# The first expert layer of a transformer block: its lower halves off GpSimd, an even pace of the gathers, and the last four output columns without a job queue

## The chip, the core and the metric

One NeuronCore of a Trainium2 chip runs the whole kernel. The metric is the device time in microseconds (us) of one execution. The engines named below are TensorE (PE, its weight loads PEld), VectorE (DVE), ScalarE (ACT), GpSimd (POOL) and SyncE (SP, which here only issues transfers).

## The reference

One block of a diffusion transformer: differential attention and gated linear attention on 256 tokens (with 256 context tokens), merged and added to x, and then an expert feed-forward, on which the change bears. All of it is float32. Cut to that part:

```
def peer_ffn(h, wq, keys, u, v):                       # h: 256 tokens x 2048
    q = (h @ wq).reshape(B, T, 8, 2, 128)
    s = einsum('bthpd,hpkd->bthpk', q, keys)           # 2 x 128 scores a head
    s1, i1 = top_k(s[..., 0, :], 16); s2, i2 = top_k(s[..., 1, :], 16)
    top_s, pos = top_k(s1[..., :, None] + s2[..., None, :], 16)
    idx = take_along_axis(i1 * 128 + i2, pos)          # 8 x 16 of 16384 experts for each token
    g = softmax(top_s)
    act = gelu(einsum('pd,ped->pe', h, u[idx]))        # first layer
    return einsum('pe,ped->pd', act * g, v[idx])       # second layer
out = x + g2 * peer_ffn(...)
```

## The kernel before

**Two ways of doing the experts.** For the first 192 tokens the kernel multiplies all 16384 rows of `u` and `v` as dense matrices (all 128 x 128 experts, 128 blocks of 128 experts), and picks the chosen experts through a matrix `A` of gains, 128 x 128 x 192, zero where an expert was not chosen. For the last 64 tokens it gathers the chosen rows: 64 tokens x 128 experts are 8192 rows, 64 gathers of 128 rows x 2048 numbers.

**The precise product.** A float32 product is made of three products of rounded parts (`fp32r`). Each weight block of 128 x 1024 is loaded by SP (`load_to`, L76) into `wraw`; ACT rounds it into the upper part `whi` (L90), and DVE or GpSimd subtracts to get the lower part `wlo` (L92): `e = nc.gpsimd if self.share(self.s) else nc.vector`. `share` is a function of the block's number. The class `Stream` splits blocks ahead of the matmuls: in the expert layers three blocks ahead, with six `wraw` buffers and four each of `whi` and `wlo`.

**The first layer.** `experts_in(i)` (L1215) does one block of 128 experts, called "one expert block" below: two weight blocks, 16 k-steps of one matmul with `whi` (L1222, 384 columns: upper and lower part of the tokens side by side) and one with `wlo` (L1223, 192 columns), and a fold of the two halves (`summed`: `low` L1234, a matmul L1236, `sum` with the gelu L1241). After every fourth k-step it calls `jobs.tick()`: four ticks in one expert block.

**The order of the work around it.** `Jobs` holds lanes of generators. Each tick takes one off the count of the first generator in every lane; at zero that generator runs to its next `yield`, whose number is the next count. So a lane's work is written into the engines' queues at a fixed pace in matmuls, and each engine then runs its own queue in order. Lanes in this layer:

- `route`: the top-16 searches on DVE, while the first expert blocks run. Until it is empty, `A` does not exist, and `W.share = lambda s: s % 4 != 0` gives three of four `wlo` to GpSimd.
- `gains` (L1264), from the moment the routing is through: 48 steps of four ticks. DVE makes `og` (L1276, four small instructions) and ACT `oh2` (L1272, L1273); two ticks later PE joins them (L1281, eight matmul records), one tick later ACT copies into `A` (L1288).
- `sparse` (`sparse_in`, L1169), from the same moment: 66 steps. Step j multiplies gathered rows j-2 with the tokens and sums (the "dot", L1173 on DVE) and issues gather j on GpSimd (L1166) into one of two `gat` buffers. Its pace is the change's second part.
- `out`: the folds. While `A` is being filled the results are parked in DRAM by an ACT transfer (`out_park`); later they are multiplied into `A` at once (`out_last`, L1251).
- `fetch` (L1253), once `A` is full: every three ticks SP loads one parked pair of blocks back (`back`, L1259) and DVE multiplies an earlier one into `A` (L1261); 38 loads.

**The second layer** runs the same 128 blocks against `v_rows` with eight accumulators: `ya[n]` (128 tokens) and `yb[n]` (64 tokens in two parts) for the four column groups n of 512. Its gathers step every six ticks. The order `vorder` ends with column groups 0 and 1 of the last two blocks, then groups 2 and 3.

**The end.** `rows_a(n)` scales `ya[n]` (L1337), adds the residual (L1338), and sends 128 rows out from SP. `rows_b(n)` scales `yb[n]` (L1345), adds its two halves by a matmul with `IJ` (L1347), adds the residual (L1348), and sends 64 rows out from ACT's queue. All take their scratch `o` from four buffers in turn. Before the change `rows_b(n)` is a generator in a job lane `end`, of which one tick advances only the first in the lane.

Of the kernel before, what the change touches and what calls it, by code (L numbers as in the profile page):

```python
# [36 lines left out]
class Stream:  # L37
# [59 lines left out]
    def next(self):  # L97
        self.split_to(self.i + self.look)
        p = self.parts.pop(self.i)
        self.i += 1  # L100
        self.flush()
        return p
# [33 lines left out]
def block_kernel(ctx, tc, a, out):  # L136
# [26 lines left out]
    W = Stream(nc, wpool, blocks, 3, 3, 2, on_pool)  # L163
    jobs = Jobs()
# [24 lines left out]
    def split(hi, lo, x):  # L189
        S.activation(hi, x, AF.Copy)  # L190
        V.tensor_tensor(lo, x, hi.bitcast(F32), OP.subtract)  # L191
# [827 lines left out]
    spool = ctx.enter_context(tc.tile_pool(name="spool", bufs=1))  # L1019
# [23 lines left out]
    nwq = [1 << 30]  # L1043
# [120 lines left out]
    def gather(pool, table, j, n):  # L1164
        gat[j] = pool.tile([128, D], F32, name="gat", bufs=n)
        G.indirect_dma_start(out=gat[j], out_offset=None, in_=table,  # L1166
                             in_offset=bass.IndirectOffsetOnAxis(ap=sidx[:, j:j + 1], axis=0))

    def sparse_in(pool, n, wait):  # L1169
        for j in range(64 + n):  # L1170
            if j >= n:
                g = gat.pop(j - n)
                V.scalar_tensor_tensor(g, g, 1.0, hrow, op0=OP.mult, op1=OP.mult, accum_out=dot[:, j - n:j - n + 1])  # L1173
            if j < 64:
                gather(pool, a["u_rows"], j, n)
            yield wait()
        S.activation(dot, dot, AF.Gelu)
        V.tensor_tensor(sg, sg, dot, OP.mult)
        yield
# [35 lines left out]
    def experts_in(i, out_):  # L1215
        acc = ps.tile([128, 512], F32, name="acc", bufs=3)
        for k in range(KT):
            if k % 8 == 0:
                hi, lo = W.next()
            c = slice((k % 8) * 128, (k % 8) * 128 + 128)  # L1220

            PE.matmul(acc[:, 0:2 * TD], hi[:, c], H2[:, k], start=(k == 0), stop=(k == KT - 1), skip_group_check=True)  # L1222
            PE.matmul(acc[:, 0:TD], lo[:, c], H2[:, k, 0:TD], start=False, stop=(k == KT - 1),  # L1223
                      skip_group_check=True)
            if k % 4 == 3:
                jobs.tick()
        W.later(lambda: jobs.add("out", summed(i, acc, out_), 0))
# [36 lines left out]
    def gains(pool, n):  # L1264
        o2, og, gp = {}, {}, {}

        def marks(t0):
            o2[t0], og[t0] = (pool.tile([128, n, 128], F32, name=x, bufs=1) for x in ("oh2", "og"))

            for t in range(n):  # L1270
                c = slice(t0 + t, t0 + t + 1)
                S.activation(o2[t0][:, t], iota, AF.Square, bias=I2N[:, c])  # L1272
            S.activation(o2[t0], o2[t0], AF.Relu, bias=one[:, 0:1], scale=-1.0)  # L1273
            for t in range(n):
                c = slice(t0 + t, t0 + t + 1)
                V.tensor_scalar(og[t0][:, t], iota, I1T[:, c], GT[:, c], op0=OP.is_equal, op1=OP.mult)  # L1276

        def join(t0):
            p = gp[t0] = sp("G").rearrange("p (t i) -> p t i", t=n)
            for t in range(n):  # L1280
                PE.matmul(p[:, t], o2[t0][:, t], og[t0][:, t], start=True, stop=True)  # L1281

        for t0 in range(0, TD, n):
            marks(t0)
            yield 2
            join(t0)
            yield 1
            S.activation(A[:, :, t0:t0 + n].rearrange("p i t -> p t i"), gp.pop(t0), AF.Copy)  # L1288
            yield 1

    A, i = None, 0
    with tc.tile_pool(name="gpool", bufs=1, side="right") as pool:
        while A is None or any(jobs.lanes.get("gains", ())):
            if A is None and not any(jobs.lanes.get("route", ())):
                tst.close()
                A = ctx.enter_context(tc.tile_pool(name="act", bufs=1)).tile([128, 128, TD], F32)
                jobs.add("gains", gains(pool, 4))
                jobs.add("sparse", sparse_in(spool, 2, lambda: 8 if any(jobs.lanes["gains"]) else 4))
                W.share = lambda s: s % 3 == 0 and s < nwq[0] + 256
            experts_in(i, out_park)  # L1300
            experts_in(i + 1, out_park)
            i += 2
        while i % 4:
            experts_in(i, out_park)
            i += 1
        W.flush()
        jobs.limit("out", 0)
# [21 lines left out]
    def part(i):  # L1329
        t = parts[i] = pool.tile([128, 2, TD, 2], F32R, name="as", bufs=2)  # L1330
        split(t[:, :, :, 0], t[:, :, :, 1], A[:, i:i + 2])

    def rows_a(n):

        d = slice(n * 512, n * 512 + 512)
        o = pool.tile([128, 512], F32, name="o", bufs=4)
        V.tensor_tensor(o, ya[n], g2r[:, d], OP.mult)  # L1337
        V.tensor_tensor(o, o, x2r[0][:, d], OP.add)  # L1338
        nc.sync.dma_start(out[0:128, d], o)

    def rows_b(n):

        d = slice(n * 512, n * 512 + 512)
        o = pool.tile([128, 512], F32, name="o", bufs=4)
        V.tensor_tensor(o, yb[n], g2r[:, d], OP.mult)  # L1345
        yield 1
        PE.matmul(yb[n][0:NS], IJ, o, start=True, stop=True, skip_group_check=True)  # L1347
        V.tensor_tensor(o[0:NS], yb[n][0:NS], x2r[1][0:NS, d], OP.add)  # L1348
        nc.scalar.dma_start(out[128:TD, d], o[0:NS])
        yield  # L1350

    part(0)
    for i, q in vorder:
        if i % 2 == 0 and q == 0 and i + 2 < 128:
            part(i + 2)
        t = parts[i // 2 * 2][:, i % 2]
        h0, h1, hb = t[:, 0:128, 0], t[:, 0:128, 1], t[:, 128:TD].rearrange("p t i -> p (t i)")
        hi, lo = W.next()
        for n in (2 * q, 2 * q + 1):
            c = slice((n % 2) * 512, (n % 2) * 512 + 512)  # L1360
            first, last = i == 0, i == 127
            PE.matmul(yb[n], hb, hi[:, c], start=first, stop=False)  # L1362
            PE.matmul(yb[n], hb, lo[:, c], start=False, stop=last)  # L1363
            PE.matmul(ya[n], h0, hi[:, c], start=first, stop=False)  # L1364
            PE.matmul(ya[n], h1, hi[:, c], start=False, stop=False)  # L1365
            PE.matmul(ya[n], h0, lo[:, c], start=False, stop=last)  # L1366
            jobs.tick()
            if last:
                jobs.add("end", rows_b(n), 0)
                jobs.tick(0)  # L1370
                rows_a(n)
    jobs.drain()


# [102 lines left out]
```

## Time and profile before

| | |
|---|---|
| median of 3 runs | 2616.52 us (2615.82 to 2617.99) |
| the profiled execution | 2615.0 us |
| its span, first to last instruction | 2613.2 us |
| busy share of the span | PE 94%, DVE 75%, ACT 50%, POOL 33% |
| mean granted PE clock | 0.968 of full speed |
| moved by transfers | 678.86 MB, mean 260 GB/s |
| first matmul of the first expert layer | 1249.1 us |
| first and last join of the gains | 1403.0 and 1685.4 us |
| first matmul of the second expert layer | 2001.3 us |

The stretches used below follow from the last three rows: 1249 to 1402 us (first expert blocks, beside the routing), 1402 to 1690 (beside the gains), 1690 to 1925 (beside the fetch and most of the gathers), 1925 to 1998 (the last blocks), then the second layer, and the end from 2590 us on. In a table by stretches each engine has its busy time and, in brackets, its instructions; PEclk is the granted clock, and the last two columns are the busy share of the 16 DMA engines and what they moved. In a table of waits a row names the waiting instruction, the one waited for, the total, the times and the longest.

### The profile page before, as it was taken

How to read it: one execution, taken by the hardware profiler on the slowest of the kernel's cores; microseconds unless marked ns; L12 is line 12 of the kernel's file. 1: busy time of each engine (PE TensorE's matmuls, PEld its weight loads, DVE VectorE, ACT ScalarE, POOL GpSimd, SP SyncE). 2: the span in 40 equal slices, each digit the busy share in tenths (PEclk: the TensorE clock that was granted, in tenths of full speed). 3: DMA queues.
4: the chain of work that ended last, by engine and by line, in shares of the span. 5: the costliest groups of instructions: out<-in, count | busy, mean ns of one | idle time of the engine just before them, and what ended most of it. 6: DMA issues, size and time to landing. Idle time of an engine off the chain costs nothing. (4 is left out here: it accounts for less than half of the span.)

```text
span 2613.2 us, 39725 instructions
## 1 busy us (share of the span) xinstructions
PE 2445.1 (94%) x15236; PEld 2204.1 (84%) x15236; DVE 1953.5 (75%) x2516; ACT 1296.2 (50%) x1947; POOL 861.9 (33%) x411
## 2 busy tenths in 40 slices
PE   6799999999999999979899999988899999999998
PEld 3477888888899999979889999978898888888886
DVE  4868888577765665469996777789964888888865
ACT  5443444333354444444447888744345444444443
POOL 4531112121202242157475333444542333223100
PEclk8799999999999999989999999999899999999999
DMA  8664555466547776675567788899987999999974
GB/s 311 221 221 169 182 186 185 127 229 210 193 137 258 259 253 211 200 208 170 163 210 260 274 288 274 288 377 376 385 316 258 362 372 378 370 376 374 359 250 153
DMA packets 196494, 678.86 MB, mean 260 GB/s; under 512 B 21840, under 2 KB 54192, under 8 KB 179152
## 3 DMA queue, kind: packets, MB, share of 16 engines
q1 hardware_dynamic: 155456, 521.36, 57.8%
q0 software_dynamic: 19008, 137.44, 13.7%
q10 hardware_dynamic: 21840, 17.53, 2.3%
q8 instruction: 119, 1.95, 0.3%
q14 instruction: 71, 0.58, 0.1%
HBM read 660.83 MB, written 11.68 MB: 257 GB/s over the span
## 5 line engine op out<-in xcount | busy, mean ns | idle before, releaser
L92 DVE TENSOR_TENSOR wlo<-wraw,whi 128x1024 fp32r<-128x1024 f32 x601 | 796.0, 1345 | 313.4 <-ACT whi L90 309.0
L90 ACT ACTIVATE whi<-wraw 128x1024 fp32r<-128x1024 f32 x824 | 852.3, 1053 | 270.0 <-PE ya L1365 53.5
L92 POOL TENSOR_TENSOR wlo<-wraw,whi 128x1024 fp32r<-128x1024 f32 x223 | 567.4, 2552 | 915.7 <-ACT whi L90 886.1
L1222 PE MATMUL acc<-H,whi 128*128 128x384 f32 x2048 | 628.3, 370 | 0.0
L1223 PE MATMUL acc<-H,wlo 128*128 128x192 f32 x2048 | 530.3, 259 | 58.9 <-POOL wlo L92 36.0
L1223 PEld LDWEIGHTS acc<-H,wlo 128*128 128x128 f32 x2048 | 404.0, 197 | 68.2 <-POOL wlo L92 41.3
L1222 PEld LDWEIGHTS acc<-H,whi 128*128 128x128 f32 x2048 | 398.1, 194 | 0.0
L214 PE MATMUL acc<-H,whi 128*128 128x256 f32 (+1 forms) x1248 | 377.8, 303 | 1.4 <-ACT whi L90 1.4
L216 PE MATMUL acc<-H,wlo 128*128 128x256 f32 (+1 forms) x1248 | 372.4, 298 | 1.6 <-DVE wlo L92 0.8
L215 PE MATMUL acc<-H,whi 128*128 128x256 f32 (+1 forms) x1248 | 371.9, 298 | 0.0
L214 PEld LDWEIGHTS acc<-H,whi 128*128 128x128 f32 x1248 | 239.8, 192 | 20.2 <-issue 12.0
L216 PEld LDWEIGHTS acc<-H,wlo 128*128 128x128 f32 x1248 | 239.8, 192 | 9.2 <-DVE wlo L92 1.2
L215 PEld LDWEIGHTS acc<-H,whi 128*128 128x128 f32 x1248 | 239.8, 192 | 5.8
L1166 POOL DMA_INDIRECT gat<-v_rows,sidx x64 | 136.8, 2138 | 322.3 <-DVE ys L1188 291.1
L389 DVE SCALAR_TENSOR_TENSOR a<-a,cb 128x1024 f32<-128x1024 f32 x128 | 188.3, 1474 | 25.4 <-DMA a<-ada 25.4
L1362 PE MATMUL yb<-whi,as 128*128 128x512 f32 x512 | 203.3, 397 | 2.6 <-DVE as L191 2.6
L1363 PE MATMUL yb<-wlo,as 128*128 128x512 f32 x512 | 203.8, 398 | 0.1
L1365 PE MATMUL ya<-whi,as 128*128 128x512 f32 x512 | 203.2, 397 | 0.0
L1364 PE MATMUL ya<-whi,as 128*128 128x512 f32 x512 | 202.5, 396 | 0.0
L1366 PE MATMUL ya<-wlo,as 128*128 128x512 f32 x512 | 202.0, 395 | 0.0
L1188 DVE SCALAR_TENSOR_TENSOR ys<-gat,sg,ys 128x2048 f32<-128x2048 f32 x63 | 148.0, 2349 | 28.5 <-DMA gat<-v_rows,sidx 28.4
L1173 DVE SCALAR_TENSOR_TENSOR gat<-gat,hrow 128x2048 f32<-128x2048 f32 x64 | 146.0, 2282 | 30.9 <-DMA gat<-u_rows,sidx 30.9
(327 smaller groups left out, 4141.2 us busy)
## 6 DMA issues: line engine op xcount, KB each, us to landing
wraw<-u SPq DMA_DIRECT2D x256, 512.0 KB
wraw<-v_rows SPq DMA_DIRECT2D x256, 512.0 KB
wraw<-w_a SPq DMA_DIRECT2D x162, 512.0 KB
a<-ada SPq DMA_DIRECT2D x128, 512.0 KB
wraw<-ada SPq DMA_DIRECT2D x64, 512.0 KB
wraw<-w_br SPq DMA_DIRECT2D x32, 512.0 KB
wraw<-w_o SPq DMA_DIRECT2D x32, 512.0 KB
wraw<-w_q SPq DMA_DIRECT2D x32, 512.0 KB
```

The lines of the kernel that those rows point to most:

```text
L90: nc.scalar.activation(hi, r, AF.Copy)
L92: e.tensor_tensor(lo, r, hi.bitcast(F32), OP.subtract)
L214: PE.matmul(acc[:, :n], hi[:, c], mh, start=(k == 0), stop=False)
L215: PE.matmul(acc[:, :n], hi[:, c], ml, start=False, stop=False)
L216: PE.matmul(acc[:, :n], lo[:, c], mh, start=False, stop=(k == nk - 1))
L1222: PE.matmul(acc[:, 0:2 * TD], hi[:, c], H2[:, k], start=(k == 0), stop=(k == KT - 1), skip_group_check=True)
L1223: PE.matmul(acc[:, 0:TD], lo[:, c], H2[:, k, 0:TD], start=False, stop=(k == KT - 1), skip_group_check=True)
L1362: PE.matmul(yb[n], hb, hi[:, c], start=first, stop=False)
L1363: PE.matmul(yb[n], hb, lo[:, c], start=False, stop=last)
L1364: PE.matmul(ya[n], h0, hi[:, c], start=first, stop=False)
L1365: PE.matmul(ya[n], h1, hi[:, c], start=False, stop=False)
L1366: PE.matmul(ya[n], h0, lo[:, c], start=False, stop=last)
```

## The change

Three edits:

1. When the gains begin, `W.share` becomes a function that is always false: from there on every `wlo` of the first expert layer is made on DVE. (In the second layer none was on GpSimd before either.)
2. `sparse_in` gets the fixed pace of 6 ticks between gathers, where it had 8 while the gains ran and 4 afterwards.
3. At the end the four generators of `rows_b` are advanced by hand: the first half of `rows_b(n)` right behind the matmuls of column group n, the second half of `rows_b(n - 1)` behind it, and only then `rows_a(n)`.

```
 def sparse_in(pool, n, wait):
     ...
-            yield wait()
+            yield wait
 ...
-                jobs.add("sparse", sparse_in(spool, 2, lambda: 8 if any(jobs.lanes["gains"]) else 4))
-                W.share = lambda s: s % 3 == 0 and s < nwq[0] + 256
+                jobs.add("sparse", sparse_in(spool, 2, 6))
+                W.share = lambda s: False
 ...
     def rows_b(n):
         ...
         V.tensor_tensor(o, yb[n], g2r[:, d], OP.mult)
-        yield 1
+        yield
         PE.matmul(yb[n][0:NS], IJ, o, start=True, stop=True, skip_group_check=True)
 ...
+    end = []
 ...
             if last:
-                jobs.add("end", rows_b(n), 0)
-                jobs.tick(0)
+                end.append(rows_b(n))
+                next(end[-1])
+                if n:
+                    next(end[n - 1])
                 rows_a(n)
+    next(end[3])
     jobs.drain()
```

GpSimd's queue, beside the gains, a gather (`gat`) and the lower parts (`wlo`) in turn; before:

```order
L1166 DMA gat<-u_rows,sidx 128x2048
L92 TENSOR_TENSOR wlo<-wraw,whi 128x1024 x2
L1166 DMA gat<-u_rows,sidx 128x2048
L92 TENSOR_TENSOR wlo<-wraw,whi 128x1024
L1166 DMA gat<-u_rows,sidx 128x2048
L92 TENSOR_TENSOR wlo<-wraw,whi 128x1024
```

and after, from the routing's two small transfers on:

```order
L1110 DMA sg<-top 64x8x8 x2
L92 TENSOR_TENSOR wlo<-wraw,whi 128x1024 x2
L1166 DMA gat<-u_rows,sidx 128x2048 x64
L1166 DMA gat<-v_rows,sidx 128x2048 x64
L1196 DMA gat<-xr 128x2048
```

68 lower parts have left GpSimd (223 before, 155 now), and nothing stands between its gathers any more.

DVE's queue in the middle of the gains (`og` is the gains' operand, `gat,dot` a dot), before:

```order
L92 TENSOR_TENSOR wlo<-wraw,whi 128x1024 x2
L1276 TENSOR_SCALAR og<-iota,I1T,GT 128x128 x4
L1173 SCALAR_TENSOR_TENSOR gat,dot<-gat,hrow 128x2048
L92 TENSOR_TENSOR wlo<-wraw,whi 128x1024
L1276 TENSOR_SCALAR og<-iota,I1T,GT 128x128 x4
L92 TENSOR_TENSOR wlo<-wraw,whi 128x1024
L1276 TENSOR_SCALAR og<-iota,I1T,GT 128x128 x4
L1173 SCALAR_TENSOR_TENSOR gat,dot<-gat,hrow 128x2048
```

and after:

```order
L92 TENSOR_TENSOR wlo<-wraw,whi 128x1024 x2
L1276 TENSOR_SCALAR og<-iota,I1T,GT 128x128 x4
L1173 SCALAR_TENSOR_TENSOR gat,dot<-gat,hrow 128x2048
L92 TENSOR_TENSOR wlo<-wraw,whi 128x1024 x2
L1276 TENSOR_SCALAR og<-iota,I1T,GT 128x128 x4
L92 TENSOR_TENSOR wlo<-wraw,whi 128x1024
L1173 SCALAR_TENSOR_TENSOR gat,dot<-gat,hrow 128x2048
L92 TENSOR_TENSOR wlo<-wraw,whi 128x1024
L1276 TENSOR_SCALAR og<-iota,I1T,GT 128x128 x4
```

Between two `og` there are now always two `wlo`, and in two of three such pieces a dot as well.

DVE's queue from the third column group on at the end (L1345, L1348: `rows_b`; L1337, L1338: `rows_a`), before:

```order
L1345 TENSOR_TENSOR o<-yb_20227,g2r 128x512
L1337 TENSOR_TENSOR o<-ya_20224,g2r 128x512
L1338 TENSOR_TENSOR o<-o,gat 128x512
L1348 TENSOR_TENSOR o<-yb_20227,gat 64x512
L1345 TENSOR_TENSOR o<-yb_20228,g2r 128x512
L1348 TENSOR_TENSOR o<-yb_20228,gat 64x512
```

and after:

```order
L1345 TENSOR_TENSOR o<-yb_20227,g2r 128x512
L1348 TENSOR_TENSOR o<-yb_20226,gat 64x512
L1337 TENSOR_TENSOR o<-ya_20223,g2r 128x512
L1338 TENSOR_TENSOR o<-o,gat 128x512
L1345 TENSOR_TENSOR o<-yb_20228,g2r 128x512
L1348 TENSOR_TENSOR o<-yb_20227,gat 64x512
L1337 TENSOR_TENSOR o<-ya_20224,g2r 128x512
L1338 TENSOR_TENSOR o<-o,gat 128x512
L1348 TENSOR_TENSOR o<-yb_20228,gat 64x512
```

The scaling of the last `yb` has moved ahead of three other instructions. The order of PE's instructions is the same in both kernels.

## The prediction

> **What bounds the kernel now.** I first cut the span into stretches by what runs beside the first expert layer, since busy shares over the whole span hide it. Whole kernel by stretches, then the L1222 matmuls alone (16 to an expert block):
>
> ```profile
> core 0: us, PE busy (x) PEld busy (x) DVE busy (x) ACT busy (x) POOL busy (x), PEclk, DMA share, GB/s
> 1402.00:1690.00 288.00, 275.76 (x1976) 270.78 (x1975) 215.71 (x303) 250.30 (x478) 106.38 (x57) 1.00 0.81 281
> 1690.00:1925.00 235.00, 200.24 (x1258) 194.99 (x1257) 206.06 (x185) 98.39 (x153) 114.56 (x66) 0.92 0.99 376
> 1925.00:1998.00 73.00, 72.87 (x505) 72.64 (x504) 35.38 (x34) 37.63 (x61) 27.12 (x13) 0.99 0.75 248
> 1998.00:2590.00 592.00, 589.03 (x2516) 484.95 (x2517) 479.21 (x384) 283.39 (x319) 137.05 (x66) 1.00 0.93 341
> ...
> 1402.00:1690.00 288.00, 231.64 (x771) 145.08 (x772) 1.00 0.81 281
> 1690.00:1925.00 235.00, 194.30 (x610) 123.63 (x610) 0.92 0.99 376
> 1925.00:1998.00 73.00, 72.20 (x245) 46.37 (x244) 0.99 0.75 248
> ```
>
> PE sets the pace in the last stretch (0.13 us idle): 245/16 = 15.3 blocks in 73 us, 4.77 us a block. Beside the gains a block takes 288/(771/16) = 5.98 us, with 12.2 us idle. From 1690 to 1925 it takes 235/(610/16) = 6.17 us; PE is idle for 34.8 us, its clock falls to 0.92, and the transfers are at 0.99. The second layer leaves 3.0 us in 592. So the room is between 1402 and 1925. Who is waited for there: the waits of 1402 to 1690 (two rows), then of 1690 to 1925:
>
> ```profile
> PE acc L1223 <- POOL wlo L92: 6.9, 8, 0.9
> PE sp L1281 <- DVE og L1276: 5.4, 15, 0.5
> ...
> POOL gat L1166 <- DVE gat L1173: 107.5, 35, 5.2
> PE acc L1223 <- POOL wlo L92: 29.1, 13, 3.1
> DVE gat L1173 <- DMA gat<-u_rows,sidx: 27.8, 13, 5.0
> PE acc L1223 <- DVE wlo L92: 5.1, 5, 1.4
> ```
>
> 29.1 of the 34.8 us are waits for a `wlo` on GpSimd. The chain of work shows why it is late, the timeline what a wait costs after it ends:
>
> ```profile
> 1742.83 1.03 POOL gat L1166
> ...
> 1743.88 2.52 POOL wlo L92
> ...
> 1741.03 0.35 PE L1223 MATMUL acc<-H,wlo 128*128 128x192 f32 x1 [3.05 <-POOL wlo L92]
> 1741.22 0.36 PE L1222 MATMUL acc<-H,whi 128*128 128x384 f32 x1
> ...
> 1742.70 0.57 PE L1222 MATMUL acc<-H,whi 128*128 128x384 f32 x1
> ```
>
> GpSimd's queue is in order: the `wlo` stands behind a gather, the gather waits for a dot to free its buffer, the dot for an earlier gather's data. At four ticks a gather that ring turns too slowly, and PE hangs on it. 1.7 us after a wait of 3.05 us the same matmul takes 0.57 us instead of 0.36. That is the second part of the loss: 38.1 blocks at 4.77 us are 182 us, so the excess is 53 us, of which 34.8 idle and some 18 slow clock.
>
> **The change, edit by edit: lower parts to DVE.** 68 leave GpSimd. What DVE pays is read where GpSimd is idle, start to start, and what it paid beside a busy GpSimd from a pair of rows:
>
> ```profile
> 1719.15 3.90 DVE L92 TENSOR_TENSOR wlo<-wraw,whi 128x1024 fp32r<-128x1024 f32 x1
> ...
> 1729.46 2.27 DVE L1173 SCALAR_TENSOR_TENSOR gat<-gat,hrow 128x2048 f32<-128x2048 f32 x1
> ...
> 1731.66 1.21 DVE L92 TENSOR_TENSOR wlo<-wraw,whi 128x1024 fp32r<-128x1024 f32 x1
> 1732.80 0.55 DVE L1251 TENSOR_TENSOR A<-A,sum 128x384 f32<-128x384 f32 x1
> 1733.27 0.55 DVE L1261 TENSOR_TENSOR A<-A,back 128x384 f32<-128x384 f32 x1
> 1733.74 1.21 DVE L92 TENSOR_TENSOR wlo<-wraw,whi 128x1024 fp32r<-128x1024 f32 x1
> ...
> 1719.61 2.35 POOL L92 TENSOR_TENSOR wlo<-wraw,whi 128x1024 fp32r<-128x1024 f32 x1
> ...
> 1434.29 1.11 DVE L1276 TENSOR_SCALAR og<-iota,I1T,GT 128x128 f32<-128x128 f32 x4
> 1435.32 2.28 DVE L1173 SCALAR_TENSOR_TENSOR gat<-gat,hrow 128x2048 f32<-128x2048 f32 x1
> ```
>
> A dot takes 2.20 us, a `wlo` 1.14, `A`'s products 0.47 each, an `og` 1.03. The 3.90 beside GpSimd's 2.35 shows DVE held until GpSimd is through, so a moved `wlo` costs 1.14 and can give back up to 2.7. After the change DVE has to do per block, beside the gains: 2 x 1.14 + 1.03 + 2/3 x 2.20 = 4.78 us; beside the fetch: 2.28 + 1.47 + 4/3 x 0.47 + 0.24 = 4.61. Both are below the 4.77 of PE, narrowly. ACT's work is the same. Queued behind a `wlo` on DVE are dots and `og`, and behind a dot GpSimd's next gather; SP's loads wait for a `wlo` to free `wraw`, and these six buffers cover a late one.
>
> Beside the gains: a join adds 0.84 us to PE (below, start to next start), so PE's floor is 4.77 + 0.84 = 5.61 against 5.98.
>
> ```profile
> 1425.49 1.08 PE L1281 MATMUL sp<-og,oh 128*128 128x128 f32 x8
> ...
> 1426.33 0.42 PE L1222 MATMUL acc<-H,whi 128*128 128x384 f32 x1
> ```
>
> If nothing waited, 48.2 blocks x 0.37 = 17.6 us would go. But `og` must be done two ticks after it is issued, and a dot (2.20 us) now stands ahead of two in three. PE's waits for it (5.4 us now) could grow by half a microsecond on 32 of 48: +16 us, which leaves a loss of a few us. Between -17 and +10 I take -6, nearer to the gain, since the 6.9 us for GpSimd go for certain and DVE has 15% of the floor free.
>
> **Even pace.** 66 steps x 6 ticks / 4 = 99 blocks, of 101.6 between 1402 and 1998 (1626 k-steps / 16), so the last dot falls within the layer and nothing spills into the next. The bytes:
>
> ```profile
> wraw<-u SPq DMA_DIRECT2D x77, 512.0 KB
> back<-park SPq DMA_DIRECT2D x38, 192.0 KB
> gat<-u_rows,sidx POOLq DMA_INDIRECT x40, 8.2
> ```
>
> Per block beside the fetch: weights 1024 KB, `back` 4/3 x 192 = 256, and gathers of 1024 KB (128 x 2048 x 4 bytes): one a block before, two thirds now. That is 2.36 MB before, at 376 GB/s 6.27 us (seen: 6.17, some blocks had no fetch), and 2.01 MB now: 5.35 us. So transfers remain the limit for the 28.5 blocks (38 x 3 ticks / 4) of the fetch, above DVE's 4.61 and PE's 4.77: 152 us, less what the weight buffers hold in reserve at the start, 0 to 8 us (6 x 512 KB at 376 GB/s); I take 4. The other 24.9 of the 53.4 blocks need 1.75 MB, at 4.77 us 366 GB/s, just below the 376: 24.9 x 4.77 = 119, and 1 for waits. Together 268 us, where 1690 to 1998 took 308: -40. Beside the gains the gathers rise from 0.5 to 0.67 a block; (1024 + 683 + 96 parked) KB in 5.85 us are 316 GB/s, which fits.
>
> The Trainium skill, "DMA: Bandwidth & Descriptors", section "Specifications", gives about 358 GB/s from HBM for one core. By it the fetch would take 2.01 MB / 358 = 5.61 us a block, 8 us more in all, and the gathers' later blocks 4.88. The row of 376 GB/s over 235 us contradicts it, so the sum goes by the row.
>
> **The end.** The last instructions:
>
> ```profile
> 2602.65 7.66 ACTq L1349 DMA_DIRECT2D out<-o  x3
> ...
> 2603.86 0.68 DVE L1345 TENSOR_TENSOR o<-yb,g2r 128x512 f32<-128x512 f32 x1
> ...
> 2606.38 0.67 DVE L1345 TENSOR_TENSOR o<-yb,g2r 128x512 f32<-128x512 f32 x1
> ...
> 2607.11 1.97 PE L1347 MATMUL yb<-o,IJ 128*64 128x512 f32 x2 [1.44 <-DVE o L1345]
> 2609.12 0.68 DVE L1348 TENSOR_TENSOR o<-yb,gat 64x512 f32<-64x512 f32 x1 [2.06 <-PE yb L1347]
> ```
>
> The last scaling (2606.38) comes at about 2603.9 after, where the third one stands now, and the matmul behind it runs beside the two instructions of `rows_a(3)`; with three more of DVE's instructions of some 0.65 us ahead of it the last add starts near 2606.4 instead of 2609.12, -2.7. Against it: its scratch buffer is that of `rows_b(1)`, sent at 2602.65, so it may wait a microsecond for that transfer. Between -3 and 0 I take -2.
>
> **Sum.** -6 - 40 - 2 = -48 from the profiled execution's 2615.0 (span 2613.2 and 1.8 around it): 2567. That execution is 1.5 below the median of the runs, so I say 2568.
>
> **The rivals.**
> - PE sets the pace everywhere: the transfers keep up beyond 376 GB/s. For it: 0.99 is a busy share, which need not mean that no more bytes fit; against it: with the gathers always waiting, 376 is all that came in 235 us. 53.4 x 4.77 = 255 (-53), gains -17, end -3: 2543.
> - Transfers cost more, as at 358 GB/s: 28.5 x 5.61 + 19 x 4.88 + 5.9 x 4.77 = 281 (-27), with -6 and -2: 2581. The row speaks against it, an uneven mix of gathers and loads for it.
> - DVE's order takes part of it back. A wait of PE for DVE's `wlo` was 5.1/5 = 1.0 us; if each of 64 dots causes 0.4 us: +26, 2594. For it DVE's 4.78 and 4.61 against 4.77; against it only 5 such waits beside 40 gathers, and splits three blocks ahead.
> - Slower: the same mechanism at its full price, 64 x 1.0 = +64 us: 2632. It decides from 48/64 = 0.75 us a dot on. Beside the gains the dot must then hold `og` past its join nearly every time.
> - The change does nothing measurable: the gathers' ring was only where PE's wait showed, and transfers hold the same 6.17 us. Against it, the bytes per block fall by 15%.
>
> **How the numbers follow.** The forecast, 2554 to 2580, 0.60; PE everywhere 0.10; dearer transfers 0.13; DVE's order 0.10; slower 0.04; nothing 0.03. 0.2% (5 us) is about what a measurement of this kernel can tell from no change. The first four are faster: 0.93; same 0.03, slower 0.04. The range 2550 to 2594 holds the forecast, the dearer transfers and most of DVE's order, and leaves out the fastest and the two last cases, under 0.2.
>
> **What would show it.** Right: no PE wait for GpSimd after 1402; a block beside the fetch near 5.2 us with the clock above 0.97, DMA share still above 0.95; the last join near 1680; the last dot some five blocks before the layer's end; a first matmul of the second layer near 1955; the end from the last `ya` matmul 2 us shorter. Wrong: PE waits for DVE's `wlo` or `og` of more than 20 us; DVE above 95% busy; ACT waiting for `wraw` in the last blocks too, or the second layer's 592 us growing.

## The result, and the profile after

The changed kernel takes 2555.16 us (median of 4 runs, 2551.56 to 2557.57), beside 2616.17 for the kernel before (4 runs): a ratio of 0.977, with a 95% interval of 0.9748 to 0.9793. The prediction was 2568, in a range of 2550 to 2594. The profiled execution took 2551.56, its span is 2549.8.

The same stretches after the change, which now begin and end earlier (first the whole kernel, then the L1222 matmuls alone):

```profile
core 0: us, PE busy (x) PEld busy (x) DVE busy (x) ACT busy (x) POOL busy (x), PEclk, DMA share, GB/s
1399.00:1666.00 267.00, 267.00 (x1941) 265.60 (x1940) 226.99 (x343) 246.08 (x473) 50.90 (x31) 1.00 0.91 326
1666.00:1836.00 170.00, 160.97 (x1093) 155.74 (x1092) 151.11 (x163) 87.61 (x134) 24.36 (x22) 1.00 1.02 386
1836.00:1935.00 99.00, 99.00 (x696) 99.00 (x695) 82.34 (x79) 53.06 (x84) 20.15 (x12) 1.00 0.97 367
...
1399.00:1666.00 267.00, 226.11 (x755) 141.85 (x754) 1.00 0.91 326
1666.00:1836.00 170.00, 155.72 (x530) 99.35 (x530) 1.00 1.02 386
1836.00:1935.00 99.00, 98.19 (x338) 63.16 (x337) 1.00 0.97 367
```

Beside the gains PE is busy without a gap, 267 of 267 us. From 1666 to 1836, beside the fetch, it is idle for 9.0 us instead of 34.8, a block takes 170/(530/16) = 5.13 us instead of 6.17, and the clock stays at 1.00. In the last blocks a block takes 99/(338/16) = 4.69 us. The waits, one row of 1399 to 1666 and the others of 1666 to 1836:

```profile
DVE wlo L92 <- ACT whi L90: 38.8, 35, 2.0
...
POOL gat L1166 <- DVE gat L1173: 142.2, 22, 8.2
DVE A L1261 <- DMA back<-park: 11.4, 24, 1.4
PE acc L1223 <- DVE wlo L92: 6.2, 11, 0.9
PE acc L1236 <- DMA wraw<-u: 2.1, 1, 2.1
```

In these stretches no engine is shown waiting for GpSimd any more. GpSimd itself still waits for dots, but nothing stands behind its gathers. DVE now waits for fetched blocks, and PE a little for DVE.

For the comparison of many runs three times are enough: first to last join of the gains (L1281), last join to the first matmul of the second layer, and from there to the end of the span. The rows of before and of the changed kernel (whose lines are one higher at the end):

```profile
L1281 PE MATMUL sp<-og,oh x384: 275/275/377, 1403.1 to 1685.5; 128*128 128x128 f32 x192
L1362 PE MATMUL yb<-whi,as x512: 392/397/632, 2001.3 to 2601.8; 128*128 128x512 f32 x171
...
L1281 PE MATMUL sp<-og,oh x384: 275/275/369, 1399.2 to 1665.6; 128*128 128x128 f32 x192
L1363 PE MATMUL yb<-whi,as x512: 392/397/795, 1939.0 to 2541.2; 128*128 128x512 f32 x171
```

Joins 282.4 us before, 266.4 after (-16.0); the rest of the layer 315.8 and 273.4 (-42.4); second layer and end 611.9 and 610.8 (-1.1). The first join comes 3.8 us earlier, but that start wanders between 1396.7 and 1406.7 in the runs below, so it is no part of the effect. The last of the three times lies between 607.1 and 612.4 in all of them, so the gain at the very end can't be read from it.

### The profile page after: what moved, and what is told of

Same layout as the page of the kernel before. It is cut to its first block, busy times and chain, and to the rows that moved or that the text cites. A ratio compares the mean times of both kernels' runs of the same rounds, so it can differ in the third digit from the quotient of the medians.

```text
span 2549.8 us, 39628 instructions
## 1 busy us (share of the span) xinstructions
PE 2427.0 (95%) x15236; PEld 2188.9 (86%) x15236; DVE 1950.9 (77%) x2584; ACT 1298.1 (51%) x1947; POOL 690.7 (27%) x343
## 4 chain that ended last, share of the span: by engine, by line
PE 66%; DVE 16%; DMA 7%; issue 2%; ACT 2%; ACTq 0%; SPq 0%; POOL 0%; DVEq 0%; POOLq 0%
PE acc L1222 10%; PE acc L214 6%; PE acc L216 6%; PE acc L215 6%; PE yb L1364 5%; PE acc L1223 5%; PE yb L1363 5%; PE ya L1366 4%; PE ya L1367 4%; PE ya L1365 4%; DMA back<-park 4%; DVE wlo L92 2%; PE acc L413 2%; PE acc L415 2%; PE acc L416 2%
## 5 line engine op out<-in xcount | busy, mean ns | idle before, releaser
L92 DVE TENSOR_TENSOR wlo<-wraw,whi 128x1024 fp32r<-128x1024 f32 x669 | 841.2, 1278 | 283.9 <-ACT whi L90 280.0
L92 POOL TENSOR_TENSOR wlo<-wraw,whi 128x1024 fp32r<-128x1024 f32 x155 | 400.7, 2594 | 786.3 <-ACT whi L90 768.3
L1222 PE MATMUL acc<-H,whi 128*128 128x384 f32 x2048 | 612.0, 364 | 0.0
L1223 PE MATMUL acc<-H,wlo 128*128 128x192 f32 x2048 | 521.6, 255 | 21.3 <-DVE wlo L92 20.9
L1223 PEld LDWEIGHTS acc<-H,wlo 128*128 128x128 f32 x2048 | 394.7, 193 | 27.9 <-DVE wlo L92 27.6
L1222 PEld LDWEIGHTS acc<-H,whi 128*128 128x128 f32 x2048 | 388.7, 190 | 0.0
L214 PEld LDWEIGHTS acc<-H,whi 128*128 128x128 f32 x1248 | 239.2, 192 | 20.3 <-issue 12.1
L216 PEld LDWEIGHTS acc<-H,wlo 128*128 128x128 f32 x1248 | 239.1, 192 | 8.4 <-DVE wlo L92 1.2
L215 PEld LDWEIGHTS acc<-H,whi 128*128 128x128 f32 x1248 | 239.3, 192 | 5.8
L1166 POOL DMA_INDIRECT gat<-v_rows,sidx x64 | 121.0, 1890 | 368.7 <-DVE ys L1188 307.1
L389 DVE SCALAR_TENSOR_TENSOR a<-a,cb 128x1024 f32<-128x1024 f32 x128 | 194.1, 1520 | 23.4 <-DMA a<-ada 23.3
L1166 POOL DMA_INDIRECT gat<-u_rows,sidx x64 | 94.3, 1474 | 409.4 <-DVE gat L1173 409.0
```

The source lines that it names most:

```text
L92: e.tensor_tensor(lo, r, hi.bitcast(F32), OP.subtract)
L214: PE.matmul(acc[:, :n], hi[:, c], mh, start=(k == 0), stop=False)
L215: PE.matmul(acc[:, :n], hi[:, c], ml, start=False, stop=False)
L216: PE.matmul(acc[:, :n], lo[:, c], mh, start=False, stop=(k == nk - 1))
```

## The experiments

All times in us; each ratio is against runs of the kernel before on the same chip. The first three times are those just defined, of each run's one profiled execution. "Part" is GpSimd's third of the lower parts, moved by one or two weight blocks. Two kernels leave out some of the work, as told where they come up.

| kernel | joins | rest of layer | second layer, end | median | ratio (95% interval) |
|---|---|---|---|---|---|
| before | 282.4 | 315.8 | 611.9 | 2616.17 | 1 |
| changed | 266.4 | 273.4 | 610.8 | 2555.16 | 0.977 (0.9748 to 0.9793) |
| changed, again | 266.4 | 272.6 | 609.0 | 2555.62 | 0.978 (0.976 to 0.9801) |
| lower parts only | 263.7 | 307.5 | 612.4 | 2589.44 | 0.9906 (0.989 to 0.9923) |
| even pace only | 263.7 | 283.6 | 609.1 | 2562.75 | 0.9819 (0.9796 to 0.9843) |
| end only | 282.4 | 316.3 | 607.1 | 2610.18 | 0.9987 (0.9976 to 0.9998) |
| without the end | 266.5 | 276.4 | 611.4 | 2556.01 | 0.978 (0.9763 to 0.9796) |
| even pace, part behind the gather | 309.6 | 284.1 | 610.6 | 2608.33 | 0.9979 (0.9968 to 0.999) |
| even pace, part two behind | 277.1 | 299.2 | 611.1 | 2591.44 | 0.9923 (0.9897 to 0.9949) |
| changed, pace 5 then 7 | 265.9 | 276.0 | 608.7 | 2553.79 | 0.9772 (0.975 to 0.9794) |
| changed, half of each fetch left out | 266.5 | 271.3 | 609.4 | 2550.12 | 0.9764 (0.9744 to 0.9783) |
| changed, fetch's products mostly left out | 266.5 | 275.6 | 609.1 | 2555.14 | 0.9783 (0.9763 to 0.9802) |
| changed, fetch from ACT's queue | 266.5 | 277.0 | 609.9 | 2555.43 | 0.9784 (0.9767 to 0.98) |

The three kernels with both of the first two edits and nothing else different in this layer (changed, changed again, without the end) show how well a profile repeats: joins within 0.1 us, the rest of the layer between 272.6 and 276.4.

**Each edit alone.** The kernel before with the lower parts moved:

```
-                W.share = lambda s: s % 3 == 0 and s < nwq[0] + 256
+                W.share = lambda s: False
```

> Edit 1 alone: every lower part on DVE once the gains begin, gathers at the old pace (8 ticks beside the gains, 4 after), the end as before. Theory (two limits: PE hung on GpSimd's queue, and behind it transfers limit the stretch): beside the gains the whole 16 us of the change come from this edit; after them the gathers at 4 ticks need 2.36 MB a block beside the fetch, at the 386 GB/s seen after the change 6.1 us, then 2.1 MB, 5.4 us, then 4.7 us: 28.5 x 6.1 + 13.5 x 5.4 + 11.4 x 4.7 = 300 us where before took 308. In all about -24 us, 2592, with PE waiting for data or for DVE instead of for GpSimd. Rival (GpSimd's queue was the whole limit): as with all edits, about -60, 2556.

2589.44: the theory's number. Beside the gains all of the gain is there (-18.7). After them the wait for GpSimd is gone, and the time is lost to data: 390 GB/s, and waits for `wlo` on DVE, which stands behind dots that wait for their gathers. From 1671 to 1853:

```profile
1671.00:1853.00 182.00, 156.50 (x1015) 147.46 (x1013) 162.09 (x171) 80.58 (x126) 40.04 (x31) 0.98 1.01 390
...
PE acc L1223 <- DVE wlo L92: 24.6, 29, 2.3
DVE gat L1173 <- DMA gat<-u_rows,sidx: 11.6, 11, 3.0
```

The pace alone:

```
-                jobs.add("sparse", sparse_in(spool, 2, lambda: 8 if any(jobs.lanes["gains"]) else 4))
+                jobs.add("sparse", sparse_in(spool, 2, 6))
```

> Edit 2 alone: gathers every 6 ticks, a third of the lower parts still on GpSimd, the end as before. Theory: the bytes fit again after the gains (5.2 us a block beside the fetch, 4.8 after), but lower parts still stand behind gathers that wait for a dot, and DVE and GpSimd still hold each other up: about -25 us, 2590, with PE waits for GpSimd between 10 and 30 us, and nothing gained beside the gains. Rival (the even pace is the whole cause): -45 or more, 2571 or less, with PE waits for GpSimd under 5 us after the gains.

2562.75: the rival's size, not the theory's. The theory was wrong on the joins, where the pace alone brings the same -18.7 although a third of the lower parts is still on GpSimd, and too small on the rest (-32.2). PE's waits between 1667 and 1846, then from 1846 to 1946:

```profile
PE acc L1223 <- DVE wlo L92: 11.2, 11, 4.4
...
PE acc L1223 <- POOL wlo L92: 1.5, 3, 0.7
```

So the even pace is the larger part of the change, with GpSimd's third at the place where this kernel has it. Why it also frees the gains, and how much depends on that place, is asked further on.

The end alone (the end of the changed kernel, all else as before):

> Edit 3 alone: the last column groups finished by hand, nothing else. Theory: the stretch from the last matmul on ya to the end of the span is 2 to 3 us shorter than before; in the time about -2, below what the runs can tell from no change. Rival (the last adds wait for their scratch buffers): under 1 us shorter.

The stretch from the last `ya` matmul to the end of the span is 2.8 us shorter (7.55 us, 2601.65 to 2609.2, instead of 10.34), as the theory had it, and no add waits for its scratch buffer. For the whole time the ratio's interval, 0.9976 to 0.9998, just leaves out no change. And both other edits together, without the end:

> Edits 1 and 2 without the end. Theory: all of the change but 2 us: about 2557. If edits 1 and 2 add up from their single runs, their sum is this run's gain; theory expects more than the sum, since each alone leaves one of the two limits in place.

2556.01. The theory wanted more than the sum of the single runs; it is less: 0.94% and 1.81% alone, 2.2% together. The table shows where: on the rest of the layer the two add up (-8.3 and -32.2 alone, -39.4 together); on the joins either one alone takes 18.7 us, and both together 15.9.

**Why the pace alone frees the gains.** GpSimd's third has a period of three weight blocks, six ticks. With six ticks to a gather both have the same period, and each gather stands at the same place beside GpSimd's lower part; with eight it came to each of three places in turn. Two kernels shift that place by one and by two weight blocks:

```
-                W.share = lambda s: s % 3 == 0 and s < nwq[0] + 256
+                W.share = lambda s: s % 3 == 1 and s < nwq[0] + 256     # the other: s % 3 == 2
```

> As the run with the even pace alone, but the third of the lower parts that GpSimd makes is moved by one block (number s % 3 == 1 instead of 0). In that run's queues each step has the order: GpSimd's lower part, dot, gather, two lower parts on DVE; here the lower part stands directly behind the gather. Theory (place in the queue: a lower part behind a gather waits for the dot, starts with DVE's next one, and then holds DVE; at the old 8 ticks one of three steps stood so, 8 of 24, and PE waited 8 times): beside the gains the 18 us gained come back and more, 265 us become 280 to 295, with some 30 waits of PE for GpSimd; in all 15 to 40 us slower than the even pace alone, 2575 to 2605. Rival (only the number of bytes a tick matters, or the even rhythm as such): no difference, 2563, no PE waits for GpSimd beside the gains.

2608.33, the joins 309.6 instead of 263.7: more than the theory's 280 to 295 us, and the whole time 3 us above its range. At the same pace, with the same bytes, the joins take 27 us longer than before the change, while the rest of the layer keeps its gain (284.1). Beside the gains PE waits 15 times for GpSimd, half of what was expected, and 29 times for `og`. Its queues on GpSimd and DVE, and PE's waits from the same time:

```profile
1458.38 0.95 POOL L1166 DMA_INDIRECT gat<-u_rows,sidx  x1 [7.38 <-PE acc L1223]
1459.35 2.39 POOL L92 TENSOR_TENSOR wlo<-wraw,whi 128x1024 fp32r<-128x1024 f32 x1
...
1455.82 2.28 DVE L1173 SCALAR_TENSOR_TENSOR gat<-gat,hrow 128x2048 f32<-128x2048 f32 x1
...
1459.29 3.55 DVE L92 TENSOR_TENSOR wlo<-wraw,whi 128x1024 fp32r<-128x1024 f32 x1 [1.18 <-ACT whi L90]
1462.76 1.10 DVE L1276 TENSOR_SCALAR og<-iota,I1T,GT 128x128 f32<-128x128 f32 x4
...
1461.80 0.36 PE L1223 MATMUL acc<-H,wlo 128*128 128x192 f32 x1 [0.83 <-POOL wlo L92]
1463.24 1.17 PE L1281 MATMUL sp<-og,oh 128*128 128x128 f32 x8 [0.22 <-DVE og L1276]
```

The gather goes out when the dot is through (1458.1), the lower part behind it starts only then, DVE's next `wlo` runs into it and takes 3.55 us, and `og` comes late behind that. (The brackets of the gather's row name PE as what released it, but that had long been done; the dot's end fits to 0.3 us.)

> The same with s % 3 == 2: a lower part of DVE between the gather and the lower part of GpSimd. Theory (place in the queue): the gather is out by then, so like the even pace alone within 6 us, 2563, hardly any PE wait for GpSimd beside the gains. Rival (any lower part on GpSimd after a gather is late): as the other shifted run, 2575 or more.

2591.44: outside the theory's 6 us. The place matters, but I had judged it by what waits behind the gather alone. What DVE pays shows the rest. DVE's `wlo` and `og` between 1405 and 1660 us, with the mean ns of one, in the kernel before, the even pace alone, the part directly behind, the part two behind, and the changed kernel:

```profile
L92 DVE TENSOR_TENSOR wlo<-wraw,whi 128x1024 fp32r<-128x1024 f32 x57 | 85.6, 1501 | 66.0 <-ACT whi L90 63.5 <-ACT A L1288 2.5
L1276 DVE TENSOR_SCALAR og<-iota,I1T,GT 128x128 f32<-128x128 f32 x172 | 64.7, 440 | 0.0
...
L92 DVE TENSOR_TENSOR wlo<-wraw,whi 128x1024 fp32r<-128x1024 f32 x61 | 75.1, 1230 | 69.1 <-ACT whi L90 59.4 <-ACT oh L1273 9.7
L1276 DVE TENSOR_SCALAR og<-iota,I1T,GT 128x128 f32<-128x128 f32 x184 | 51.1, 345 | 0.0
...
L92 DVE TENSOR_TENSOR wlo<-wraw,whi 128x1024 fp32r<-128x1024 f32 x52 | 93.6, 1801 | 38.2 <-ACT whi L90 32.0 <-ACT A L1288 6.2
L1276 DVE TENSOR_SCALAR og<-iota,I1T,GT 128x128 f32<-128x128 f32 x152 | 74.2, 549 | 0.0
...
L1276 DVE TENSOR_SCALAR og<-iota,I1T,GT 128x128 f32<-128x128 f32 x174 | 87.7, 572 | 0.0
L92 DVE TENSOR_TENSOR wlo<-wraw,whi 128x1024 fp32r<-128x1024 f32 x58 | 70.7, 1218 | 42.8 <-ACT whi L90 42.8
...
L92 DVE TENSOR_TENSOR wlo<-wraw,whi 128x1024 fp32r<-128x1024 f32 x91 | 111.3, 1224 | 37.9 <-ACT whi L90 36.1
L1276 DVE TENSOR_SCALAR og<-iota,I1T,GT 128x128 f32<-128x128 f32 x180 | 50.0, 349 | 0.0
```

GpSimd's part can hold DVE at two places of its queue. Directly behind the gather, it holds both `wlo` and `og`; two behind, it holds `og` (572 ns instead of 345), which PE's joins wait for; only before the gather does it fall beside a dot, which it does not slow (2.28 us in every run). The joins follow: 309.6, 277.1, 263.7, and 282.4 for the mixture before (the mean of the three is 283.5). So the pace alone frees the gains by a good place that it happens to fix, and the first edit by emptying the queue.

The good place is not the same everywhere. In the rest of the layer the part directly behind the gather costs nothing (284.1 us, 283.6 with the even pace alone), but two behind it costs 15.6 us (299.2), and there PE waits for GpSimd nearly as long as the 29.1 us of before (1690 to 1970 us):

```profile
POOL gat L1166 <- DVE gat L1173: 122.4, 26, 5.6
...
PE acc L1223 <- POOL wlo L92: 27.5, 23, 2.6
```

So of the 32.2 us that the even pace brings there, about half hangs on the place too. The gather ahead of GpSimd's part again waits for dots; why it does so longer with this place is not shown.

**Why both edits take 2.7 us more on the joins than either alone.** All six profiles with the first two edits and a pace of 6 have 266.4 or 266.5. A join in DVE's and PE's rows of the changed kernel, then the next join:

```profile
1507.01 1.23 DVE L92 TENSOR_TENSOR wlo<-wraw,whi 128x1024 fp32r<-128x1024 f32 x1 [0.82 <-ACT whi L90]
1508.15 2.28 DVE L1173 SCALAR_TENSOR_TENSOR gat<-gat,hrow 128x2048 f32<-128x2048 f32 x1
...
1510.36 1.22 DVE L92 TENSOR_TENSOR wlo<-wraw,whi 128x1024 fp32r<-128x1024 f32 x1
1511.49 1.11 DVE L1276 TENSOR_SCALAR og<-iota,I1T,GT 128x128 f32<-128x128 f32 x4
...
1511.98 1.22 PE L1281 MATMUL sp<-og,oh 128*128 128x128 f32 x8
...
1516.37 1.12 DVE L1276 TENSOR_SCALAR og<-iota,I1T,GT 128x128 f32<-128x128 f32 x4
...
1517.72 1.08 PE L1281 MATMUL sp<-og,oh 128*128 128x128 f32 x8
```

The first `og` has a dot between its two lower parts and ends at 1512.60, 0.6 us after the join began; the second ends before its join. PE is not shown idle: the wait lies inside the join's matmuls. This is so in 15 of the 48 joins, each with `wlo`, dot, `wlo` ahead of `og`, and from the start of the matmul before a join to that of the one behind it, all 48 together take 2.7 us more than at the usual 0.92 us each. With either edit alone that order does not occur.

**What limits the blocks beside the fetch now.** First a pace that takes gathers out of that stretch:

> The changed kernel with gathers every 5 ticks beside the gains and every 7 after. Theory (transfers limit the fetch stretch alone): there a block needs 1024 + 4/7 x 1024 + 256 KB = 1.91 MB, at 386 GB/s 4.95 us instead of 5.13 seen, 28.5 x 0.18 = 5 us; beside the gains 1.99 MB in 5.56 us are 357 GB/s and fit. So 5 us faster than the changed kernel, about 2550. Rival (DVE binds there: dots 4/7 x 2.2 us are only 0.2 us a block less, and beside the gains DVE has 5.07 of 5.56 us): no faster, or slower by PE waits for og.

2553.79 beside 2555.62: no difference, and the fetch takes as long (139.1 us between its first and last load, 139.3 in the changed kernel). 5% fewer bytes a block moved at a lower rate: 368 GB/s between 1690 and 1820 us, where 389 moved in the changed kernel. Bytes alone, as the theory has it, are not the limit.

Then two kernels, one without half of the fetch's bytes, one without most of DVE's work with it:

```
# the first kernel
-                nc.sync.dma_start(back[i], park[i:i + 2].rearrange("a p t -> p a t"))
+                nc.sync.dma_start(back[i][:, 0], park[i])
...
-                V.tensor_tensor(A[:, i - 4:i - 2], A[:, i - 4:i - 2], back.pop(i - 4), OP.mult)
+                t = back.pop(i - 4)[:, 0:1].to_broadcast([128, 2, TD])
+                V.tensor_tensor(A[:, i - 4:i - 2], A[:, i - 4:i - 2], t, OP.mult)
# the second kernel
-                V.tensor_tensor(A[:, i - 4:i - 2], A[:, i - 4:i - 2], back.pop(i - 4), OP.mult)
+                V.tensor_tensor(A[:, i - 4:i - 2, 0:8], A[:, i - 4:i - 2, 0:8], back.pop(i - 4)[:, :, 0:8], OP.mult)
```

> The changed kernel, but each fetch loads only the first of its two parked blocks (96 KB instead of 192), and the multiplication on DVE uses it for both, at the same size. This leaves out half of the parked results. Theory (bytes limit the stretch of the fetch): 1.88 MB a block instead of 2.01, at 386 to 392 GB/s 4.8 to 4.9 us a block instead of 5.1; between 1690 and 1820 us about 430 k-steps of PE instead of 407 to 411, DVE's waits for the fetched blocks gone. Rival (DVE's own work limits it): under 415 k-steps, as now.

> The changed kernel with the whole fetch loaded, but DVE's product with it over 8 of 192 tokens only (about 0.15 us instead of 0.56). This leaves out most of that product. Theory (bytes limit the stretch): 405 to 415 k-steps between 1690 and 1820, as now, DVE's waits for fetched blocks longer by what the products are shorter. Rival (DVE's work of 4.6 us a block, with its waits, limits it): 4/3 x 0.4 = 0.5 us a block less, 430 k-steps or more.

The L1222 matmuls between 1690 and 1820 us and DVE's wait for fetched blocks there; the changed kernel, half of each fetch, short products:

```profile
1690.00:1820.00 130.00, 119.65 (x407) 76.24 (x406) 1.00 1.02 389
DVE A L1261 <- DMA back<-park: 10.8, 22, 1.4
...
1690.00:1820.00 130.00, 124.85 (x422) 80.01 (x421) 0.99 0.99 372
DVE A L1262 <- DMA back<-park: 9.4, 14, 1.7
...
1690.00:1820.00 130.00, 121.74 (x409) 77.68 (x409) 0.99 1.03 393
DVE A L1261 <- DMA back<-park: 22.9, 30, 2.2
```

In all they take 2550.12 and 2555.14 us (2 runs each); by their ratios in the table neither whole time can be told from the changed kernel's. DVE's work is not the limit: 0.4 us off each product becomes 12 us more waiting, and PE's 409 k-steps lie within the 402 to 411 that the three kernels with the same layer show there. Fewer bytes help, but by less than the theory had: 422 k-steps instead of 430, the rest of the layer 271.3 us, only 1.3 us under the shortest of the three, and DVE's waits stay.

> The changed kernel with the fetch issued from ScalarE's queue instead of SyncE's, where it stands behind the weight loads. Theory (bytes): DVE's 11 us of waits for fetched blocks shrink, since these no longer queue behind 512 KB loads, but the weights then come later by as much; no more than 2 us faster or slower, 2555. Rival (a late fetched block holds DVE in its queue, and DVE then PE: place in the queue, not bytes): those waits go, and PE's 6 us of waits for DVE with them, about 6 us faster, 2549.

2555.43, no faster, as the theory had it, though DVE's waits for fetched blocks did not shrink (10.6 us against 10.8); and in the fetch it is slower (393 k-steps instead of 407), for a reason neither had: now ACT's rounding waits behind a fetch that waits for DVE to free its buffer, 43.4 us in 18 times. So for the 0.4 us a block above PE's pace DVE's work is excluded, and the transfers remain: fewer bytes of the fetch gave some of it back, fewer bytes of the gathers nothing. Whether the rest is the lateness of the fetched blocks is not shown and stays open.

## Why the prediction was right, and where its sizes were off

The measured 2555 lies 13 us below the forecast of 2568 and 12 above the 2543 of its rival "PE everywhere", so the number alone does not choose between them; the stretches do.

- **The rest of the layer: -40 forecast, -42.4 seen.** The wait for GpSimd is gone, the clock with it is back at 1.00, and a block beside the fetch takes 5.13 us where the sum had (152 - 4)/28.5 = 5.2. The step "transfers remain the limit" holds in direction (a block takes longer than PE's pace, the transfers' share is 1.02, DVE's work is excluded by the short products). Its price, bytes over a fixed rate, is shown in part only: the rate was 386 instead of 376 GB/s, and with 5% fewer bytes it fell instead of the time. That the size came out so near is thus partly luck. The 358 GB/s of the Trainium skill ("DMA: Bandwidth & Descriptors", "Specifications") are there a stack's 716 GB/s divided by two cores; here one core ran the kernel, and it moved 386, and 390 with the lower parts alone, so for one core alone they were no limit.
- **Beside the gains: -6 forecast, -16.0 seen.** This is the term that was mis-sized. The working had its bound right (-17.6 if nothing waits) and then took 10 us off, since a dot ahead of `og` might make PE wait for it. That wait exists, but in 15 joins and for 2.7 us in all. What made `og` late before was mostly GpSimd's lower part: of the 16 joins that began before their `og` was done, 15 had a dot and a `wlo` ahead of it, and in eight of these that `wlo` was held (3.5 us), in seven one of `og`'s four pieces (3.2 us). With the even pace alone the same order stands 15 times ahead of an `og`, nothing is held, and none is late. The pieces of `og` took 440 ns in the mean, 349 after. The row of a `wlo` at 3.90 us stood in the prediction; I counted that relief for DVE's load and not for the lateness of `og`. The working also calls DVE's 4.78 us a block "below the 4.77 of PE", which it is not; beside the gains it stands against the floor of 5.61.
- **The end: -2 forecast.** From the last `ya` matmul to the last add it was 6.26 us (2602.86 to 2609.12) and is 3.51, -2.75, the same as with this edit alone; the wait for the scratch buffer did not come. The last `ya` matmul before, then the rows after:

```profile
2602.86 0.40 PE L1366 MATMUL ya<-wlo,as 128*128 128x512 f32 x1
...
2542.21 0.40 PE L1367 MATMUL ya<-wlo,as 128*128 128x512 f32 x1
...
2542.60 0.69 DVE L1338 TENSOR_TENSOR o<-o,gat 128x512 f32<-128x512 f32 x1
2543.21 0.68 DVE L1345 TENSOR_TENSOR o<-yb,g2r 128x512 f32<-128x512 f32 x1
...
2543.95 1.07 PE L1347 MATMUL yb<-o,IJ 128*64 128x512 f32 x2 [0.34 <-DVE o L1345]
...
2545.72 0.68 DVE L1348 TENSOR_TENSOR o<-yb,gat 64x512 f32<-64x512 f32 x1
```

- **The edits' shares** were not told apart rightly: the moved lower parts looked like the heart of the change, since PE's wait named GpSimd. Alone they bring 0.9%, the pace alone 1.8%. The wait named the queue; what turned it too slowly after the gains was the pace, together with the place of GpSimd's part: at the even pace, two behind, the wait is back.
- **The rivals.** DVE's order showed only in the 2.7 us on the joins; behind them PE waits 6.2 us for DVE in place of 5.1, in 11 times. PE everywhere came true in two of three stretches, not beside the fetch. The last dot (1910.6 us, some five blocks before the layer's end) and the clock came as listed; the last join at 1665.6 and the first matmul of the second layer at 1939 came 14 and 16 us earlier than listed.

## What to carry to other kernels

When an engine's queue mixes short helpers with instructions that wait (a gather for its buffer), look at what stands behind the waiting one; emptying the queue, or fixing a place where nothing is hit, gained the same on the joins here. Two periodic patterns on one queue that do not divide each other pass through every bad place in turn; the same pace at another offset moved the joins from 264 to 310 us. A place that is good in one stretch can be bad in another, so try the offsets as well as the pace. When two edits remove the same stall, single runs add up to more than the change: measure by stretch before giving each its share.

## What the runs showed of the hardware

- The granted clock stayed at 1.00 from 1666 to 1836 us with 9.0 us of idle PE in waits of at most 2.1 us, and was 0.92 before with 34.8 us in waits up to 3.1 us. As much idle time in shorter waits left it at 1.00: with the part directly behind the gather PE is idle for 34.1 us of its joins, in waits of at most 1.2 us.

```profile
1399.00:1709.00 310.00, 275.89 (x1939) 266.18 (x1937) 262.96 (x312) 246.29 (x472) 105.81 (x63) 1.00 0.83 283
```

- An `og` of 128 columns can be held by GpSimd's subtraction as a `wlo` can: 572 ns in the mean with the part two behind, 345 with the part before the gather. The dots were not held in any run: each took 2.27 to 2.29 us, also the 34 that ran beside GpSimd's part with the even pace alone.
- A matmul that waits for part of its input need not show as idle time: the longest matmul of the late joins took 369 ns in the changed kernel, and 296 and 308 with either edit alone, while PE counted as busy throughout.
